# Query/key products token-major with 512 moving columns, turned afterwards by transposes

## The chip, the core and the metric

The kernel runs on one core of a Trainium2 chip. The engines are named as in the profile: PE (TensorE matmuls; PEld its weight loads), DVE (VectorE), ACT (ScalarE), POOL (GpSimd) and SP (SyncE, which issues most DMAs). Matmuls accumulate in PSUM, in banks of 128 partitions by 512 f32. The metric is the device time of one execution in microseconds; lower is better.

## What is computed

Two layers of a streaming encoder on 512 tokens of width 2048. Each layer normalises its input, multiplies it by one wide input projection, and splits the columns between a gated linear attention (GLA) group and a chunked softmax attention group of 8 heads:

```python
def hybrid_layer(x, w_in, w_out, ...):
    h = rmsnorm(x, g_pre)
    z = h @ w_in
    gq, gk, gv, gg, ga, aq, ak, av, ag = split_columns(z)
    ...
    o_att = chunk_band_attention(aq, ak, av, rel_bias)   # 8 heads of 128
    o_att = rmsnorm(o_att, g_att) * jax.nn.silu(ag)
    y = jnp.concatenate([o_gla, o_att], axis=-1) @ w_out
    return x + rmsnorm(y, g_post)
```

The change concerns `aq` and `ak`, the queries and keys of the softmax attention, 1024 columns each.

## The kernel before

**Two-term operands.** Each operand of a product is a rounded high part and a low rest, and each product is three matmuls: high by high, high by low, low by high. `split` (lines 108 to 110) makes the two parts of a tile: ACT writes the rounded copy (line 109), DVE the difference (line 110). `split_scaled` (from line 112) does so with a factor (lines 118 and 119).

**Blocks and pairs.** The weight columns are cut into blocks of 512. A query/key block holds the 256 query columns of two heads and then their 256 key columns; `QK01`, `QK23`, `QK45` and `QK67` are the four. `fast_gemm` (line 372) multiplies all 512 tokens by a pair of blocks with a scheme of seven products on quarters (Strassen's kind) in place of eight. `PAIRS[1]` is (QK01, QK23) and `PAIRS[2]` is (QK45, QK67), so each layer has two query/key calls and the kernel four (lines 1108 and 1109).

**Jobs.** A call runs 28 jobs: products P1 to P7, each over four chunks c of the 2048 inputs. A job is one chunk of 512 inputs, and `kk` runs over its two halves. For each job the weights are loaded, combined with another block where the product asks for it (DVE, lines 234, 236, 256), and split (ACT line 240, DVE line 250); `ahead()` prepares the coming jobs before a finished quarter is handed over. Then come the job's matmuls. After a product's last chunk, `copies` moves its accumulators out of PSUM (ACT, line 395), or `finished` hands a quarter over: `combine` returns a function that adds or subtracts two tiles on DVE (line 400) in place, in an `ev` buffer. P3, P7 and P2 hand over with a combination; P4 hands over its accumulator itself. Each handover comes in two parts of 128x512. The order of the last chunks in a call is P1, P5, P6, P3, P7, P2, P4; P7's is job 20 and P4's job 28.

**Two layouts.** With `feature_major=True`, which only the two query/key calls set, the weights are stationary and the tokens move: each job has 24 matmuls with 256 moving columns (line 435; 2 halves, 4 groups of 128 features, 3 terms). The result has features on partitions, as the attention scores need it, and the two parts of a quarter are its queries and its keys (`b` in `qk_consume`). In the other layout the tokens are stationary and the weights move: 12 matmuls with 512 moving columns (line 445; 2 halves, 2 token tiles, 3 terms), and the two parts are token tiles `t`.

**Query/key handover.** `qk_consume` (line 1087) takes a part, settles its combination, and splits it at 128x512 into the four tiles of its block: query high and low (scaled by `-QS`), key high and low. The last part of a block starts the attention of its two heads, by appending `attend` to `tasks`.

**Order of work.** `tasks` holds generators that run a step at a time; `delayed` holds functions that run after a count of steps. After each job, `Pace` advances them by `rate` steps (2.1 in the query/key calls). So attention runs in small steps between the jobs: scores (lines 976 to 978), the softmax (DVE 982, ACT 986), transposes of the probabilities (line 998, copied out by ACT line 1001 and DVE line 1003), the mix with the values (line 1015), and a last turn (line 1040). The instructions made in this order are then ordered for each engine by a planner, which keeps the dependencies, may put ready work of lower priority first, and assigns buffers from the pools. The pool `ps_ax` has four PSUM banks for everything that is not a product's accumulator (`aux()`), the pool of the accumulators four, and the `t2` temporaries have eight buffers.

**The product after it.** `PAIRS[3]` (linear attention's keys and queries) already runs token-major, and `transpose_q` turns its query quarters by four transposes through the identity (line 1119) with two ACT copies (line 1121).

Of the kernel before, what the change touches and what calls it, by code (L numbers as in the profile page):

```python
# [15 lines left out]
P = 128  # L16
# [10 lines left out]
QS = 128 ** -0.5  # L27
# [9 lines left out]
def hybrid_trunk(  # L37
# [14 lines left out]
    nc = tc.nc  # L52
# [38 lines left out]
    def aux():  # L91
        return ps_ax.tile([P, 512], F32, tag="ax", name=nm("ax"))
# [15 lines left out]
    def split(hi, lo, src):  # L108
        nc.scalar.copy(hi, src)
        return nc.vector.tensor_tensor(out=lo, in0=src, in1=hi.bitcast(F32), op=ALU.subtract).ins  # L110

    def split_scaled(hi, lo, src, scale, first=False):
        if first:
            first_high.append(
                nc.vector.tensor_scalar(out=hi, in0=src, scalar1=scale, scalar2=None, op0=ALU.mult).ins
            )
        else:
            nc.scalar.activation(hi, src, AF.Copy, scale=scale)
        nc.vector.scalar_tensor_tensor(
            out=lo, in0=src, scalar=scale, in1=hi.bitcast(F32), op0=ALU.mult, op1=ALU.subtract  # L120
        )
# [197 lines left out]
    def until(cond):  # L319
        while not cond():  # L320
            assert tasks or delayed
            pump(1)
# [46 lines left out]
    A = {}  # L369
    roles = ["XY", "YX"]  # L370

    def fast_gemm(l, pair, consume, rate=0.0, skip=0, feature_major=False, after=None, end=False, lag=0, ops=A, prod=None, acc=None):
        b0 = pair[0]
        gates = b0 == AG1
        wide = N1 if gates else W
# [42 lines left out]
        def matmuls(job, k, c, ts):  # L418
            a = job.a
            if a is None:  # L420
                key = {"P1": (0, 0, c), "P2": (1, 0, c), "P4": (1, 1, c)}.get(k) or (LEFT[k], c)
                until(lambda: key in ops)
                a = ops[key]
            out_ps = acc[target[k]]
            fresh = k in starts and c == 0
            apart = end and (k, c) in (("P7", 3), ("P4", 0))
            for kk, some in [(kk, (t,)) for t in ts for kk in range(2)] if apart else [(kk, ts) for kk in range(2)]:
                if feature_major:
                    for ft in range(4):
                        f = slice(ft * P, (ft + 1) * P)  # L430
                        tok = slice(kk * 256, (kk + 1) * 256)
                        dst = out_ps[ft // 2][:, (ft % 2) * 256 : (ft % 2 + 1) * 256]
                        terms = ((job.wh, 0), (job.wh, 1), (job.wl, 0))
                        for m, (lhs, part) in enumerate(terms):
                            nc.tensor.matmul(  # L435
                                dst, lhs[:, kk, f], a[:, part, tok],
                                start=(fresh and kk == 0 and m == 0 and ft % 2 == 0),
                                stop=(c == 3 and kk == 1 and m == 2), skip_group_check=True,
                            )
                else:  # L440
                    for t in some:
                        tok = slice(kk * 256 + t * P, kk * 256 + (t + 1) * P)
                        terms = ((0, job.wh), (0, job.wl), (1, job.wh))
                        for m, (part, rhs) in enumerate(terms):
                            last_mm[0] = nc.tensor.matmul(  # L445
                                out_ps[t], a[:, part, tok], rhs[:, kk, :],
                                start=(fresh and kk == 0 and m == 0),
                                stop=(c == 3 and kk == 1 and m == 2), skip_group_check=True,
                            ).ins

        for k, c in prod:
            if k == "P2" and (end or gates) and c == 0 or k == "P5" and parted and c == 0:
# [32 lines left out]
    def settled(src, comb):  # L485
        return src if comb is None else comb()
# [293 lines left out]
    def layer(l):  # L780
# [182 lines left out]
        class Head:  # L963
# [70 lines left out]
            def turn(self):  # L1034
                c, kk = self.hd // 2, self.hd % 2
                if kk == 0:
                    turned[c] = slot("g16", [2, 512], F32R)
                ps = aux()
                for t in range(NT):
                    nc.tensor.transpose(ps[:, t * P : (t + 1) * P], self.sg[:, t, :], ident)  # L1040
# [17 lines left out]
        def attend(hd, qk):  # L1058
            heads = {"a": Head(hd, qk, 0), "b": Head(hd + 1, qk, 1)}

            def turn(h):
                h.turn()
                if h.hd % 2:
                    heads_done.add(hd)

            for _ in range(5 if hd == HEADS[0] else 0):
                yield
            for step in ORDER:
                if step == "-":
# [12 lines left out]
                yield  # L1082
# [4 lines left out]
        def qk_consume(p):  # L1087
            sets = {}

            def f(j, h, b, src, comb):  # L1090
                if j not in sets:
                    if (p, j) == (1, 0):
                        until(lambda: 2 in heads_done)
                    sets[j] = [slot(tag, [2, 512], F32R) for tag in QKT[p, j]]
                z = settled(src, comb).rearrange("p (f n) -> p f n", f=2)
                hs = slice(h * 256, (h + 1) * 256)
                hi, lo = sets[j][2 * b][:, :, hs], sets[j][2 * b + 1][:, :, hs]
                if b == 0:
                    split_scaled(hi, lo, z, -QS)
                else:  # L1100
                    split(hi, lo, z)
                if h and b:
                    tasks.append(attend(4 * p + 2 * j, sets[j]))
            return f

        load_bias(0)
        load_bias(1)
        fast_gemm(l, PAIRS[1], qk_consume(0), rate=2.1, feature_major=True)
        fast_gemm(l, PAIRS[2], qk_consume(1), rate=2.1, feature_major=True)

        until(lambda: 0 in heads_done)
        tasks.insert(0, forget_gate_decay())
# [480 lines left out]
```

## Time and profile before

| | before |
|---|---|
| median of 3 runs | 1597.54 us (1596.91 to 1597.74) |
| profiled execution | 1597.99 us |
| its span, first to last instruction | 1596.1 us |
| TensorE clock granted, mean | 0.999 |
| matmuls | 9102 |
| query/key stage, layer 0 | about 176 to 369 us |
| query/key stage, layer 1 | about 967 to 1159 us |

In a row of a group stand the line, the engine, the operation, the tile it writes and the ones it reads, the shapes and the count; after the bar the group's busy time in us (overlaps counted once), the mean of one in ns, and the idle time of the engine just before them with what ended it. In a row of the timeline stand the start and the length in us; `x2` are two merged instructions, and a bracket gives idle time before it and its releaser. A row of the stretches gives, after the bounds and the length, each engine's busy time with the count of instructions, the granted clock, the share of the DMA engines and GB/s.

### The profile page before, as it was taken

The page shows a single profiled execution, that of the slowest core. Times are in us where ns is not written, and L with a number is a line of the kernel's source. Part 1 is how long each engine was busy: PE and PEld are TensorE (multiplying, and loading weights), DVE is VectorE, ACT ScalarE, POOL GpSimd, SP SyncE. Part 2 cuts the span into 40 slices and gives each one's busy share as a digit, 9 for nine tenths or more (in the row PEclk, how much of TensorE's full clock was granted, in tenths as well). Part 3 has the DMA queues.
Part 4 walks back from the last instruction along what each step waited for, and adds up shares of the span by engine and source line. Part 5 has one row for each costly group of instructions (what it writes and reads, how often), then busy time and mean ns, then how long its engine had stood idle before and what let it go on. Part 6 is the DMA issues. An engine that isn't in the chain of part 4 may idle for free.

```text
span 1596.1 us, 25037 instructions
## 1 busy us (share of the span) xinstructions
PE 1584.9 (99%) x9102; PEld 1369.8 (86%) x9102; DVE 1279.6 (80%) x1697; ACT 920.9 (58%) x1535; POOL 140.6 (9%) x222
## 2 busy tenths in 40 slices
PE   9999999999999999999999999999999999999998
PEld 7998999998888777888888899999988887788886
DVE  5978777678787877998989878775887878689887
ACT  7554445657464556664686456455675655566654
POOL 0220000001000011100122000000010000101001
PEclk9999999999999999999999999999999999999999
DMA  9798686685858769689879998847869586686887
GB/s 354 232 408 308 224 305 210 218 297 193 287 205 270 280 214 315 221 298 404 302 260 352 377 337 314 283 155 266 296 223 313 174 331 239 219 302 234 337 307 199
DMA packets 137739, 441.45 MB, mean 277 GB/s; under 512 B 15364, under 2 KB 27908, under 8 KB 137584
## 3 DMA queue, kind: packets, MB, share of 16 engines
q1 hardware_dynamic: 119952, 377.86, 66.2%
q0 software_dynamic: 17376, 61.70, 11.0%
q8 instruction: 72, 1.18, 0.3%
q14 instruction: 51, 0.42, 0.1%
q10 hardware_dynamic: 288, 0.30, 0.1%
HBM read 380.23 MB, written 61.62 MB: 277 GB/s over the span
## 4 chain that ended last, share of the span: by engine, by line
PE 91%; DVE 4%; DMA 3%; issue 1%; ACT 1%; POOLq 0%; DVEq 0%; ACTq 0%
PE mm L445 53%; PE mm L435 18%; PE mm L358 7%; PE ax L445 4%; DMA raw<-in_w_dram 3%; PE ax L1015 2%; DVE wl L250 2%; PE ax L1201 1%; PE ax L998 1%; PE ax L1173 1%; PE ax L978 1%; PE ax L977 1%; PE ax L976 1%; PE ax L1293 0%; DMA sa<-S 0%
## 5 line engine op out<-in xcount | busy, mean ns | idle before, releaser
L445 PE MATMUL mm<-wh,sa 128*128 128x512 f32 (+1 forms) x1600 | 506.1, 389 | 0.6 <-ACT wh L240 0.5
L240 ACT CAST wh<-H 128x1024 fp32r<-128x1024 f32 (+1 forms) x240 | 245.1, 1023 | 198.8 <-PE mm L445 86.2
L445 PEld LDWEIGHTS mm<-wh,sa 128*128 128x128 f32 x1600 | 298.1, 188 | 70.8 <-issue 6.9
L240 ACT CAST wh<-raw 128x1024 fp32r<-128x1024 f32 (+2 forms) x237 | 236.2, 1002 | 205.0 <-PE mm L445 84.2
L250 DVE TENSOR_TENSOR wl<-H,wh 128x1024 fp32r<-128x1024 f32 (+1 forms) x240 | 284.7, 1188 | 85.5 <-PE mm L445 37.8
L250 DVE TENSOR_TENSOR wl<-raw,wh 128x1024 fp32r<-128x1024 f32 (+2 forms) x237 | 272.8, 1156 | 55.4 <-PE mm L435 20.3
L445 PE MATMUL mm<-wl,sa 128*128 128x512 f32 (+1 forms) x800 | 310.3, 388 | 0.1
L435 PE MATMUL mm<-sa,wh 128*128 128x256 f32 x1280 | 237.7, 286 | 0.0
L445 PE MATMUL mm<-wh,a 128*128 128x512 f32 (+1 forms) x672 | 217.2, 389 | 0.0
L435 PEld LDWEIGHTS mm<-sa,wh 128*128 128x128 f32 x1280 | 200.5, 192 | 0.4
L435 PE MATMUL mm<-sa,wl 128*128 128x256 f32 x640 | 181.5, 284 | 0.1
L445 PEld LDWEIGHTS mm<-wl,sa 128*128 128x128 f32 x800 | 150.4, 188 | 29.5 <-DVE wl L250 0.9
L234 DVE TENSOR_TENSOR H<-H,raw 128x1024 f32<-128x1024 f32 (+1 forms) x136 | 161.4, 1189 | 1.5 <-DMA raw<-in_w_dram 0.9
L445 PEld LDWEIGHTS mm<-wh,a 128*128 128x128 f32 x672 | 125.1, 188 | 24.9
L445 PE MATMUL mm<-wl,a 128*128 128x512 f32 (+1 forms) x336 | 130.8, 390 | 0.5 <-DVE wl L250 0.5
L435 PEld LDWEIGHTS mm<-sa,wl 128*128 128x128 f32 x640 | 122.5, 192 | 0.4 <-DVE wl L250 0.3
L445 PE MATMUL mm<-wh,g 128*128 128x512 f32 (+1 forms) x416 | 120.5, 367 | 0.0
L489 POOL TENSOR_TENSOR sm<-sm,mhalf 128x2 f32<-128x2 f32 (+2 forms) x40 | 47.9, 1197 | 663.7 <-DVE sm L1025 364.9
L395 ACT COPY ev<-mm 128x512 f32<-128x512 f32 (+1 forms) x112 | 64.1, 572 | 57.4 <-PE mm L445 42.2
L435 PE MATMUL mm<-a,wh 128*128 128x256 f32 x512 | 94.8, 286 | 0.0
L236 DVE TENSOR_TENSOR raw<-H,raw 128x1024 f32<-128x1024 f32 (+1 forms) x52 | 61.5, 1184 | 35.8 <-DMA raw<-in_w_dram 35.6
L445 PEld LDWEIGHTS mm<-wh,g 128*128 128x128 f32 x416 | 75.4, 188 | 13.3 <-ACT ev L395 0.6
(276 smaller groups left out, 2436.3 us busy)
## 6 DMA issues: line engine op xcount, KB each, us to landing
raw<-in_w_dram SPq DMA_DIRECT2D x287, 512.0 KB, 5.2
sa<-S SPq DMA_DIRECT2D x188, 512.0 KB, 4.5
H<-in_w_dram SPq DMA_DIRECT2D x56, 512.0 KB, 5.0
sa<-A SPq DMA_DIRECT2D x48, 512.0 KB, 6.0
sa<-oS SPq DMA_DIRECT2D x32, 512.0 KB, 5.7
S<-g POOLq DMA_DIRECT2D x30, 512.0 KB, 8.0
raw<-in_w_ag_dram SPq DMA_DIRECT2D x32, 264.0 KB, 4.1
oS<-g POOLq DMA_DIRECT2D x16, 512.0 KB, 5.1
```

What stands on the lines that cost most here:

```text
L234: nc.vector.tensor_tensor(out=h, in0=h, in1=r, op=ALU.add)
L236: nc.vector.tensor_tensor(out=r, in0=h, in1=r, op=ALU.subtract)
L240: last_cast[0] = nc.scalar.copy(self.wh[:, z, :], src[:, z, :]).ins
L250: last_low[0] = nc.vector.tensor_tensor(out=self.wl[:, z, :], in0=self.src[:, z, :], in1=self.wh[:, z, :].bitcast(F32), op=ALU.subtract).ins
L358: nc.tensor.matmul(pss[o], a(part, kk, o) if callable(a) else a[:, part, t], rhs[:, kk, :], start=(i == 0 and kk == 0 and m == 0), stop=(i ...
L395: last_copy[0] = nc.scalar.copy(e, src[t]).ins
L435: nc.tensor.matmul(dst, lhs[:, kk, f], a[:, part, tok], start=(fresh and kk == 0 and m == 0 and ft % 2 == 0), stop=(c == 3 and kk == 1 and ...
L445: last_mm[0] = nc.tensor.matmul(out_ps[t], a[:, part, tok], rhs[:, kk, :], start=(fresh and kk == 0 and m == 0), stop=(c == 3 and kk == 1 ...
L489: nc.gpsimd.tensor_tensor(out=out_r, in0=v, in1=mhalf[:, : v.shape[-1]], op=ALU.pow)
L976: nc.tensor.matmul(ps[:, :n], self.qh[:, t], self.kh[:, :n], start=True, stop=False)
L977: nc.tensor.matmul(ps[:, :n], self.qh[:, t], self.kl[:, :n], start=False, stop=False)
L1015: nc.tensor.matmul(o, self.pt[i][:, j * P : (j + 1) * P], av[hd // 4, j // 2][:, j % 2, (hd % 4) * P : (hd % 4 + 1) * P], start=(j == 0), ...
```

## The change

The feature-major layout is taken out of `fast_gemm`; the query/key calls use the token-major one. In `qk_consume`, `f` now receives a token tile `t` of a quarter: with a combination it runs it, without one ACT copies the accumulator to a `t2` tile. It then delays `turn` by `1 + t` steps. `turn` takes an `ax` bank, turns the tile by four transposes of 128x128, and splits the query half and the key half of the result, 128x256 each, straight from PSUM. The last turn of a block starts its attention.

```diff
@@ fast_gemm, matmuls @@
-                if feature_major:
-                    for ft in range(4):
-                        f = slice(ft * P, (ft + 1) * P)
-                        tok = slice(kk * 256, (kk + 1) * 256)
-                        dst = out_ps[ft // 2][:, (ft % 2) * 256 : (ft % 2 + 1) * 256]
-                        terms = ((job.wh, 0), (job.wh, 1), (job.wl, 0))
-                        for m, (lhs, part) in enumerate(terms):
-                            nc.tensor.matmul(
-                                dst, lhs[:, kk, f], a[:, part, tok],
...
+                for t in some:
+                    tok = slice(kk * 256 + t * P, kk * 256 + (t + 1) * P)
+                    terms = ((0, job.wh), (0, job.wl), (1, job.wh))
+                    for m, (part, rhs) in enumerate(terms):
+                        last_mm[0] = nc.tensor.matmul(
+                            out_ps[t], a[:, part, tok], rhs[:, kk, :],
...
@@ qk_consume @@
-            def f(j, h, b, src, comb):
+            def turn(j, h, t, z):
                 if j not in sets:
-                    if (p, j) == (1, 0):
-                        until(lambda: 2 in heads_done)
                     sets[j] = [slot(tag, [2, 512], F32R) for tag in QKT[p, j]]
-                z = settled(src, comb).rearrange("p (f n) -> p f n", f=2)
-                hs = slice(h * 256, (h + 1) * 256)
-                hi, lo = sets[j][2 * b][:, :, hs], sets[j][2 * b + 1][:, :, hs]
-                if b == 0:
-                    split_scaled(hi, lo, z, -QS)
-                else:
-                    split(hi, lo, z)
-                if h and b:
+                ps = aux()
+                for i in range(4):
+                    nc.tensor.transpose(ps[:, i * P : (i + 1) * P], z[:, i * P : (i + 1) * P], ident)
+                tok = slice((2 * h + t) * P, (2 * h + t + 1) * P)
+                for b in range(2):
+                    hi, lo = sets[j][2 * b][:, :, tok], sets[j][2 * b + 1][:, :, tok]
+                    y = ps[:, b * 256 : (b + 1) * 256].rearrange("p (f n) -> p f n", f=2)
+                    if b == 0:
+                        split_scaled(hi, lo, y, -QS)
+                    else:
+                        split(hi, lo, y)
+                if h and t:
                     tasks.append(attend(4 * p + 2 * j, sets[j]))
+
+            def f(j, h, t, src, comb):
+                if j not in sets and (p, j) == (1, 0):
+                    until(lambda: 2 in heads_done)
+                if comb is None:
+                    z = t2()
+                    nc.scalar.copy(z, src)
+                else:
+                    z = comb()
+                delayed.append([1 + t, lambda: turn(j, h, t, z)])
             return f
...
-        fast_gemm(l, PAIRS[1], qk_consume(0), rate=2.1, feature_major=True)
-        fast_gemm(l, PAIRS[2], qk_consume(1), rate=2.1, feature_major=True)
+        fast_gemm(l, PAIRS[1], qk_consume(0), rate=2.1)
+        fast_gemm(l, PAIRS[2], qk_consume(1), rate=2.1)
```

More of the change, by code (lines that the diff above doesn't have):

```diff
@@ L370, in hybrid_trunk, with fast_gemm @@
     roles = ["XY", "YX"]
-    def fast_gemm(l, pair, consume, rate=0.0, skip=0, feature_major=False, after=None, end=False, lag=0, ops=A, prod=None, acc=None):
+    def fast_gemm(l, pair, consume, rate=0.0, skip=0, after=None, end=False, lag=0, ops=A, prod=None, acc=None):
         b0 = pair[0]
@@ L427, in matmuls @@
             for kk, some in [(kk, (t,)) for t in ts for kk in range(2)] if apart else [(kk, ts) for kk in range(2)]:
-                if feature_major:
-                    for ft in range(4):
-                        f = slice(ft * P, (ft + 1) * P)
-                        tok = slice(kk * 256, (kk + 1) * 256)
-                        dst = out_ps[ft // 2][:, (ft % 2) * 256 : (ft % 2 + 1) * 256]
-                        terms = ((job.wh, 0), (job.wh, 1), (job.wl, 0))
-                        for m, (lhs, part) in enumerate(terms):
-                            nc.tensor.matmul(
-                                dst, lhs[:, kk, f], a[:, part, tok],
-                                start=(fresh and kk == 0 and m == 0 and ft % 2 == 0),
-                                stop=(c == 3 and kk == 1 and m == 2), skip_group_check=True,
-                            )
-                else:
[L441 to L449, printed above, removed]
+                for t in some:
[4 more added lines that the diff above has]
+                            out_ps[t], a[:, part, tok], rhs[:, kk, :],
+                            start=(fresh and kk == 0 and m == 0),
+                            stop=(c == 3 and kk == 1 and m == 2), skip_group_check=True,
+                        ).ins
         for k, c in prod:
@@ L1088, in qk_consume @@
             sets = {}
-            def f(j, h, b, src, comb):
+            def turn(j, h, t, z):
                 if j not in sets:
-                    if (p, j) == (1, 0):
-                        until(lambda: 2 in heads_done)
                     sets[j] = [slot(tag, [2, 512], F32R) for tag in QKT[p, j]]
-                z = settled(src, comb).rearrange("p (f n) -> p f n", f=2)
-                hs = slice(h * 256, (h + 1) * 256)
-                hi, lo = sets[j][2 * b][:, :, hs], sets[j][2 * b + 1][:, :, hs]
-                if b == 0:
-                    split_scaled(hi, lo, z, -QS)
-                else:
-                    split(hi, lo, z)
-                if h and b:
-                    tasks.append(attend(4 * p + 2 * j, sets[j]))
+                ps = aux()
[10 more added lines that the diff above has]
+                if h and t:
+                    tasks.append(attend(4 * p + 2 * j, sets[j]))
+            def f(j, h, t, src, comb):
[4 more added lines that the diff above has]
+                    nc.scalar.copy(z, src)
+                else:
+                    z = comb()
+                delayed.append([1 + t, lambda: turn(j, h, t, z)])
             return f
```

## The prediction

> **What bounds the kernel now.** First the busy times and the clock on the page:
>
> ```profile
> PE 1584.9 (99%) x9102; PEld 1369.8 (86%) x9102; DVE 1279.6 (80%) x1697; ACT 920.9 (58%) x1535; POOL 140.6 (9%) x222
> PEclk9999999999999999999999999999999999999999
> ```
>
> PE is busy for 99% of the span at the full granted clock. A busy PE proves little by itself, because the profile models the ends of its matmuls, so the chain of work that ended last comes next:
>
> ```profile
> PE 91%; DVE 4%; DMA 3%; issue 1%; ACT 1%; POOLq 0%; DVEq 0%; ACTq 0%
> ```
>
> Ninety-one per cent of the chain is PE. The third view is the busy time by stretch; the first two rows are the query/key stages of the two layers, the only places the change touches:
>
> ```profile
> core 0: us, PE busy (x) PEld busy (x) DVE busy (x) ACT busy (x) POOL busy (x), PEclk, DMA share, GB/s
> 176.00:369.00 193.00, 191.55 (x1584) 190.44 (x1583) 141.16 (x207) 104.71 (x194) 7.62 (x10) 1.00 0.71 247
> 967.00:1159.00 192.00, 191.93 (x1588) 190.76 (x1587) 144.66 (x211) 106.60 (x198) 11.38 (x17) 1.00 0.73 257
> ```
>
> PE idles 1.5 us in the first and 0.1 us in the second, while DVE works 73 to 75% of the time, ACT 54 to 56%, and the DMA engines 0.71 to 0.73. So here PE's instructions set the time, and what the change is worth is how many PE instructions it drops and adds, each at its pace from start to start, and not at its printed duration.
>
> **Term 1, the products.** These are the groups of line 435:
>
> ```profile
> L435 PE MATMUL mm<-sa,wh 128*128 128x256 f32 x1280 | 237.7, 286 | 0.0
> L435 PE MATMUL mm<-sa,wl 128*128 128x256 f32 x640 | 181.5, 284 | 0.1
> L435 PE MATMUL mm<-a,wh 128*128 128x256 f32 x512 | 94.8, 286 | 0.0
> L435 PE MATMUL mm<-a,wl 128*128 128x256 f32 x256 | 72.3, 284 | 0.0
> ```
>
> The counts add up to 2688: 4 pairs of blocks, 28 jobs each, so 112 jobs of 24 matmuls. Line 445 does a job with 12 matmuls of 512 columns. The 286 ns is one matmul from its start to the modelled end, and neighbours overlap. The pace is read from the timeline, from its first and last row over a stretch without gaps; first line 435, then line 445 in an undisturbed stretch, then line 445 beside running attention:
>
> ```profile
> 195.81 0.40 PE L435 MATMUL mm<-sa,wh 128*128 128x256 f32 x2
> ...
> 202.64 0.40 PE L435 MATMUL mm<-sa,wh 128*128 128x256 f32 x2
> ```
>
> ```profile
> 139.65 0.39 PE L445 MATMUL mm<-wh,sa 128*128 128x512 f32 x1
> ...
> 146.91 0.39 PE L445 MATMUL mm<-wh,sa 128*128 128x512 f32 x1
> ```
>
> ```profile
> 458.35 0.63 PE L445 MATMUL mm<-wh,sa 128*128 128x512 f32 x2
> ...
> 460.66 0.39 PE L445 MATMUL mm<-wh,a 128*128 128x512 f32 x1
> ...
> 462.74 0.39 PE L445 MATMUL mm<-wl,a 128*128 128x512 f32 x1
> ...
> 463.65 0.39 PE L445 MATMUL mm<-wh,a 128*128 128x512 f32 x1
> ```
>
> From 195.81 to 202.64 start 57 matmuls: 6.83 / 57 = 119.8 ns. From 139.65 to 146.91 start 32: 226.9 ns. Beside attention ten start in 2.31 us (231 ns), a little later four in 0.91 us (228 ns). So 512 columns cost less than twice 256, because each matmul carries a charge that doesn't shrink with its columns. A job now costs 24 x 119.8 = 2875 ns. With 12 matmuls it costs 2723 ns at 226.9 and 2772 ns at 231. Over 112 jobs that saves 17.1 us at the quiet pace and 11.6 us at the slow one. I take 228 ns, nearest the quiet row, because no attention runs in the first 19 of each layer's 56 query/key jobs and beside attention both paces occur: 112 x (2875 - 2736) = **15.6 us saved**.
>
> The Trainium skill, page "TensorE: Matmul & The Clock Gate", section "Back-to-back issue gap", gives N/2.4 + 2.5 ns for warm matmuls, so 109.2 and 215.8 ns. By it the job would save 24 x 109.2 - 12 x 215.8 = 31 ns, 3.5 us in all as an estimate, and the change would lose. The rows above disagree: the charge beyond N/2.4 is about 13 ns here, at both widths, and the rows decide.
>
> **Term 2, the transposes.** Each pair hands over 8 halves of quarters (4 quarters, 2 token tiles), so `turn` runs 32 times with 4 transposes, 128 in all. The same operation, four turns of 128x128 f32 through the identity between line-435 matmuls, stands here:
>
> ```profile
> 337.70 0.29 PE L435 MATMUL mm<-sa,wl 128*128 128x256 f32 x1
> 337.83 0.60 PE L1040 MATMUL ax<-cst,sg 128*128 128x128 f32 x4
> 338.18 0.49 PE L435 MATMUL mm<-a,wh 128*128 128x256 f32 x2
> 338.51 0.28 PE L435 MATMUL mm<-a,wl 128*128 128x256 f32 x1
> ```
>
> Three line-435 matmuls and the four transposes lie between 337.70 and 338.51: 0.81 - 3 x 0.12 = 0.45 us for the four. (The next matmul's record starts early, at 338.18, but the one after it is late by the same; only the stretch over both counts.) 32 x 0.45 = **14.4 us added**.
>
> **Term 3, ACT and DVE.** The operands were split straight from the quarter, at 128x512; now they are split from the turned tile as two halves of 128x256, and the last quarter, which needs no combination, is first copied by ACT. The first four rows are today's splits in the first layer's stage, the fifth the copy of an accumulator, the last two are 128x256 work out of PSUM elsewhere:
>
> ```profile
> L118 ACT ACTIVATE g<-ev 128x512 fp32r<-128x512 f32 x6 | 3.8, 627 | 5.6 <-DVE ev L400 5.6
> L109 ACT CAST g<-ev 128x512 fp32r<-128x512 f32 x6 | 3.7, 621 | 2.4 <-DVE ev L400 2.4
> L119 DVE SCALAR_TENSOR_TENSOR g<-ev,g 128x512 fp32r<-128x512 f32 x6 | 4.0, 674 | 0.0
> L110 DVE TENSOR_TENSOR g<-ev,g 128x512 fp32r<-128x512 f32 x6 | 4.1, 684 | 0.0
> L395 ACT COPY ev<-mm 128x512 f32<-128x512 f32 x12 | 7.0, 582 | 7.4 <-PE mm L435 7.4
> L1121 ACT ACTIVATE g<-ax 128x256 f32<-128x256 f32 x16 | 5.0, 384 | 0.0
> L1188 DVE SCALAR_TENSOR_TENSOR g<-g,a_end,ax 128x256 f32<-128x256 f32 x56 | 26.8, 479 | 2.0
> ```
>
> Per pair ACT goes from 8 x 0.62 = 5.0 us to 16 x 0.38 + 2 x 0.58 = 7.3, and DVE from 8 x 0.68 = 5.4 to 16 x 0.48 = 7.7. That is 4.6 us more on each in a stage of 193 us, where ACT has 88 us free and DVE 52. I cost it at nothing; the products of PE hide it. Without that cover it would cost at most these 9.2 us in both layers.
>
> **The new waits.** The transposes wait for the combination on DVE (line 400) or the copy on ACT, which wait for the quarter's last matmul. PE takes its matmuls in the order that the planner fixed, so whatever matmuls of the next job come after the transposes in that order stand behind them while they wait. The nearest row is the same pattern in the key/query product that follows: combination, four transposes, split.
>
> ```profile
> L1119 PE MATMUL ax<-cst,ev 128*128 128x128 f32 x32 | 4.5, 272 | 0.0
> ```
>
> Eight such groups of four, no idle time before any. Against it stands the one stall of the stage, 1.45 us of PE:
>
> ```profile
> 325.71 1.23 DVE L256 TENSOR_TENSOR H<-H,raw 128x1024 f32<-128x1024 f32 x1 [4.71 <-DMA raw<-in_w_dram]
> ...
> 331.29 0.55 DVE L1003 COPY t<-ax 128x384 f32<-128x384 f32 x1
> ...
> 331.99 0.91 PE L1015 MATMUL ax<-g,t 128*128 128x128 f32 x6 [1.45 <-DVE t L1003]
> ```
>
> A weight block landed late, DVE waited 4.7 us with everything behind it, and PE stood before attention matmuls whose input DVE had not copied. So a new wait is bounded by nothing and 1.45 us; I take nothing, by the nearest row (the same pattern), and keep the other end.
>
> Each turned tile also takes one of the four `ax` banks for about two ACT and two DVE reads (1.7 us). If banks run short, attention's steps come later while PE has products to run: no cost on PE. No DMA moves, and the loads of the next jobs are issued ahead of the handover as before; a job with its share of transposes is 2736 + 129 = 2865 ns against 2875, so the weights have the same time to land. `turn` starts attention one step later; its work is unchanged.
>
> **The sum.** -15.6 + 14.4 = -1.2 us. The profiled execution took 1597.99 us (span 1596.1 and 1.9 around it), 0.45 above the median of the runs. Off the median: 1597.5 - 1.2 = **1596.3 us**. With 226.9 ns the sum is -2.7 (1594.8), with 231 ns +2.8 (1600.3). About 0.2%, 3.2 us, is what a measurement of this kernel can tell from no change.
>
> **Rivals.**
>
> - *Faster.* The quiet pace holds beside attention (-2.7), and the 1.45 us stall goes, since the steps around it shift; the second layer's stage, with the same code, idles only 0.1 us. -4.1: 1593.4. For: that row. Against: 231 ns beside attention, and nothing in the change removes late weights.
> - *Slower: DVE late at the turns.* Quarters finish where P7 and P2 prepare weights on DVE from just-landed blocks, the place of the quoted stall. Each turn caught costs 1.45 us. With -1.2 from the work, four of the 32 turns bring it past +3.2; at five it is -1.2 + 7.3: 1603.6. For: the stall exists, and 32 new places can catch it. Against: one stall among the many waits of attention on DVE and ACT today, and none at line 1119.
> - *Halving the count doesn't pay.* If a 512-column matmul cost two of 256 in this stage (239.6 ns), the transposes would be all that's left: +14.4, 1611.9. Against: no row above reaches 239.6. The skill's formula quoted above comes close to this case, and the trace doesn't bear it out.
>
> **How the numbers follow.** Forecast 0.60, faster 0.18, late turns 0.20, no saving 0.02. So faster by over 0.2% 0.18, within 0.2% 0.60, slower 0.22. The range runs from 1592.5, just past the faster case, to 1604.0, through late turns at its price of five; it leaves out more than five late turns and no saving, and covers the paces from 226.9 to 231.
>
> **What would show it.** Line 435 gone and line 445 up by 1344 matmuls of 512 columns, at 227 to 231 ns in these stages; 128 new 128x128 transposes, about 0.45 us for each four; idle PE before them near 0; the two stages together 1 to 3 us shorter. Idle time before the transposes put down to DVE would show the second rival; a pace near 240 ns the third. A change of more than 3 us outside the two stages would mean that I missed a way in which they reach the rest.

## The result, and the profile after

| | before | after |
|---|---|---|
| median, measured side by side (6 runs each) | 1597.78 us (1596.91 to 1600.03) | 1603.93 us (1602.95 to 1606.34) |
| ratio to before | 1 | 1.0037 [1.0025, 1.0050] |
| span of the profiled execution | 1596.1 us | 1604.6 us |

The changed kernel is slower by 0.37%, some 6 us, where no change that can be told (-1.2 us) was forecast. Its page shows the busy times and the chain that ended last:

```profile
PE 1587.9 (99%) x7886; PEld 1310.8 (82%) x7886; DVE 1282.6 (80%) x1729; ACT 926.8 (58%) x1575; POOL 142.2 (9%) x222
PE 91%; DVE 5%; issue 1%; DMA 1%; ACT 1%; SPq 0%; POOLq 0%; DVEq 0%; ACTq 0%
```

PE still shows 99% and 91%: as read from the page, nothing has happened. There are 9102 - 7886 = 1216 matmuls fewer, which is 1344 product matmuls fewer and 128 transposes more. What the changed query/key stages hold also reads as forecast. The timeline of PE in a stretch without attention (first and last row), and the groups of the first layer's stage (176 to 369 us):

```profile
188.70 0.62 PE L432 MATMUL mm<-wh,sa 128*128 128x512 f32 x2
...
205.70 0.62 PE L432 MATMUL mm<-wh,sa 128*128 128x512 f32 x2
```

```profile
L1082 PE MATMUL ax<-cst,ev 128*128 128x128 f32 x44 | 6.6, 272 | 0.0
...
L119 DVE SCALAR_TENSOR_TENSOR g<-ax,g 128x256 fp32r<-128x256 f32 x12 | 4.8, 405 | 0.5 <-ACT g L118 0.5
L118 ACT ACTIVATE g<-ax 128x256 fp32r<-128x256 f32 x12 | 4.6, 380 | 2.8 <-PE ax L1082 2.8
```

Between the two starts lie 75 matmuls: 17.00 / 75 = 226.7 ns, the quiet pace. The transposes have no idle time put down in front of them.

So where did the time go? The products are the same work in both kernels if a 256-column one is counted as half. So the stages can be set side by side by the start of each stage's first product, found by counting:

```
first product of           before    after   after - before
query/key pair 1, layer 0   176.4     176.7    +0.3
query/key pair 2, layer 0   263.5     261.1    -2.4
key/query product, layer 0  368.9     360.3    -8.6
value product, layer 0      460.7     454.1    -6.5
product after it, layer 0   549.7     553.1    +3.4
key/query product, layer 1 1159.3    1155.2    -4.1
value product, layer 1     1251.1    1249.1    -2.0
product after it, layer 1  1340.1    1348.1    +8.0
span                       1596.1    1604.6    +8.4
```

The -8.6 is mostly not a gain: attention, which runs between the products, is later in the changed kernel and is done in the later stages. Work moved out of one stage comes back in another. Only where attention is over, at the product after the value product, can the two be compared. There the changed kernel is 3.4 us late in layer 0 and 8.0 in both layers together, and from there on the two kernels run in step. (The profiled execution of the changed kernel, 1606.34 us, is the slowest of its six; by the medians the loss is 6.2 us.) The loss shows in the head of the value stage. The stretches of before, then of after:

```profile
core 0: us, PE busy (x) PEld busy (x) DVE busy (x) ACT busy (x) POOL busy (x), PEclk, DMA share, GB/s
454.00:480.00 26.00, 26.00 (x143) 22.31 (x142) 24.25 (x39) 14.97 (x36) 1.03 (x1) 1.00 0.42 147
1249.00:1275.00 26.00, 26.00 (x138) 22.15 (x137) 23.89 (x35) 15.20 (x35) 1.24 (x2) 1.00 0.40 136
```

```profile
454.00:480.00 26.00, 24.14 (x143) 20.25 (x142) 23.16 (x47) 17.80 (x51) 2.19 (x3) 1.00 0.41 146
1249.00:1275.00 26.00, 24.14 (x143) 20.24 (x142) 23.16 (x47) 17.80 (x51) 2.19 (x3) 1.00 0.42 148
```

PE has no idle time before and 1.86 us after, in each layer, at the full clock and with the DMA engines at 0.41 to 0.42. The timeline of PE in that window shows what it idles between:

```profile
471.08 0.39 PE L432 MATMUL mm<-wh,a 128*128 128x512 f32 x1
471.31 0.33 PE L963 MATMUL ax<-g,g 128*128 128x384 f32 x1
...
473.03 0.33 PE L985 MATMUL ax<-cst,t 128*128 128x128 f32 x1 [0.47 <-DVE sm L969]
...
475.33 0.49 PE L1002 MATMUL ax<-g,t 128*128 128x128 f32 x2
476.75 1.16 PE L1002 MATMUL ax<-g,t 128*128 128x128 f32 x8 [0.93 <-ACT t L988]
...
478.37 0.94 PE L1002 MATMUL ax<-g,t 128*128 128x128 f32 x6
479.06 0.48 PE L432 MATMUL mm<-wh,sa 128*128 128x512 f32 x1
```

From 471.31 to 479.06 PE runs no product at all, only the tail of attention (scores, transposes, mix), whose steps wait for one another through DVE and ACT. The printed gaps understate it: between the starts at 475.33 and 476.75 two matmuls ran, 0.2 us of work in 1.4. The product that comes at 479.06 is the value stage's second one. The row on DVE that ends just ahead of it stands first here, the same instruction of the kernel before second, and the first product of the changed kernel's value stage (PE) third:

```profile
477.27 1.28 DVE L1139 TENSOR_TENSOR t<-mm,g 128x512 f32<-128x512 f32 x2
```

```profile
474.50 1.28 DVE L1140 TENSOR_TENSOR t<-mm,g 128x512 f32<-128x512 f32 x2
```

```profile
454.13 0.39 PE L432 MATMUL mm<-wh,a 128*128 128x512 f32 x1
```

The DVE instruction reads P4's quarter of the key/query product out of the accumulators (`mm`), multiplies it by the decay and writes it to a `t2` tile (`t`). Until it has run, two of the four accumulator banks stay taken. The value stage's first product has the other two, and its second one must wait. Before, the instruction starts 474.5 - 460.7 = 13.8 us after the first product of the stage; after, 477.3 - 454.1 = 23.2 us after it.

The same shape stands at the head of the key/query stage, where the new copy of P4's quarter comes late. PE, then ACT:

```profile
360.05 0.39 PE L432 MATMUL mm<-wh,sa 128*128 128x512 f32 x1
```

```profile
373.35 0.38 ACT L118 ACTIVATE g<-ax 128x256 fp32r<-128x256 f32 x1 [0.71 <-PE ax L1082]
374.17 1.05 ACT L240 CAST wh<-H 128x1024 fp32r<-128x1024 f32 x1 [0.43 <-PE mm L432]
375.12 1.07 ACT L1099 COPY t<-mm 128x512 f32<-128x512 f32 x2
```

P4's last matmul starts at 360.05, and the copy of its result at 375.12, 15 us later, though ACT had idle time in between (0.71 and 0.43 us here). It too writes a `t2` tile. Three suspects follow from this: the `ax` banks, the `t2` tiles, and the accumulators held meanwhile.

### The profile page after: what moved, and what is told of

Same layout as the page of the kernel before. It is cut to its first block, busy times and chain, and to the rows that moved or that the text cites. A ratio compares the mean times of both kernels' runs of the same rounds, so it can differ in the third digit from the quotient of the medians.

```text
span 1604.6 us, 22662 instructions
## 1 busy us (share of the span) xinstructions
PE 1587.9 (99%) x7886; PEld 1310.8 (82%) x7886; DVE 1282.6 (80%) x1729; ACT 926.8 (58%) x1575; POOL 142.2 (9%) x222
## 3 DMA queue, kind: packets, MB, share of 16 engines
q0 software_dynamic: 17376, 61.70, 10.9%
## 4 chain that ended last, share of the span: by engine, by line
PE 91%; DVE 5%; issue 1%; DMA 1%; ACT 1%; SPq 0%; POOLq 0%; DVEq 0%; ACTq 0%
PE mm L432 71%; PE mm L358 6%; PE ax L432 4%; PE ax L1002 2%; DVE wl L250 1%; PE ax L1200 1%; PE ax L985 1%; PE ax L1172 1%; PE ax L1082 1%; DVE H L234 1%; PE ax L963 1%; DMA raw<-in_w_dram 1%; PE ax L965 1%; PE ax L964 1%; DVE g L110 0%
## 5 line engine op out<-in xcount | busy, mean ns | idle before, releaser
L432 PE MATMUL mm<-wh,sa 128*128 128x512 f32 (+1 forms) x2240 | 712.3, 390 | 0.8 <-ACT wh L240 0.5
L432 PEld LDWEIGHTS mm<-wh,sa 128*128 128x128 f32 x2240 | 416.6, 188 | 94.6 <-issue 8.1
L432 PE MATMUL mm<-wl,sa 128*128 128x512 f32 (+1 forms) x1120 | 435.4, 389 | 2.2 <-DVE wl L250 2.2
L432 PE MATMUL mm<-wh,a 128*128 128x512 f32 (+1 forms) x928 | 302.3, 391 | 0.0
L432 PEld LDWEIGHTS mm<-wl,sa 128*128 128x128 f32 x1120 | 210.4, 188 | 44.2 <-DVE wl L250 3.9
L432 PEld LDWEIGHTS mm<-wh,a 128*128 128x128 f32 x928 | 172.2, 188 | 33.9
L432 PE MATMUL mm<-wl,a 128*128 128x512 f32 (+1 forms) x464 | 181.4, 391 | 0.5 <-DVE wl L250 0.5
L234 DVE TENSOR_TENSOR H<-H,raw 128x1024 f32<-128x1024 f32 (+1 forms) x136 | 161.3, 1188 | 2.0 <-DMA raw<-in_w_dram 1.0
L432 PEld LDWEIGHTS mm<-wl,a 128*128 128x128 f32 x464 | 87.2, 188 | 17.6 <-DVE wl L250 0.7
L432 PEld LDWEIGHTS mm<-wh,g 128*128 128x128 f32 x416 | 75.2, 188 | 13.7 <-ACT wh L240 0.9
L432 PE MATMUL mm<-wl,g 128*128 128x512 f32 (+1 forms) x208 | 75.8, 366 | 0.0
L256 DVE TENSOR_TENSOR H<-H,raw 128x1024 f32<-128x1024 f32 (+1 forms) x44 | 51.6, 1175 | 28.0 <-DMA raw<-in_w_dram 27.6
L240 ACT CAST wh<-g 128x1024 fp32r<-128x1024 f32 x36 | 37.9, 1060 | 31.3 <-PE mm L432 14.9
```

Of the source, the lines that this page charges most:

```text
L234: nc.vector.tensor_tensor(out=h, in0=h, in1=r, op=ALU.add)
L240: last_cast[0] = nc.scalar.copy(self.wh[:, z, :], src[:, z, :]).ins
L256: nc.vector.tensor_tensor(out=h, in0=h, in1=self.src, op=ALU.add)
L432: last_mm[0] = nc.tensor.matmul(out_ps[t], a[:, part, tok], rhs[:, kk, :], start=(fresh and kk == 0 and m == 0), stop=(c == 3 and kk == 1 ...
```

## The experiments

Times are medians; a ratio is to the kernel before, run beside it on the same chip, with its 95% interval.

**The turns taken out.** Each turned tile is replaced by the unturned one, so the 128 transposes and their banks are left out, queries and keys stay token-major, and the scores are those of other operands.

```diff
-                ps = aux()
-                for i in range(4):
-                    nc.tensor.transpose(ps[:, i * P : (i + 1) * P], z[:, i * P : (i + 1) * P], ident)
...
-                    y = ps[:, b * 256 : (b + 1) * 256].rearrange("p (f n) -> p f n", f=2)
+                    y = z[:, b * 256 : (b + 1) * 256].rearrange("p (f n) -> p f n", f=2)
```

> The changed kernel without its 128 transposes and without the ax banks they take: the halves are split at 128x256 from the settled quarter itself, unturned, so the scores are those of other operands, with the same instructions. Theory held back (the turned tiles hold attention back, by their banks or the extra hop, and its tail then stalls PE at the head of the value stage): the 14.4 us of transposes go and the stall of about 8 to 10 us of both layers with them, so about 1580 us, and the first scores start about 2 us earlier. Rival, order (the planner's order is worse for any change of the products, whatever the turns do): only the 14.4 us go, about 1589.5, and the value stages stay at 99 us.

Measured: 1581.54 us beside 1597.94, ratio 0.9899 [0.9883, 0.9916]. This is what the theory expected. The products alone are 16.4 us faster (by the interval of the ratio, 13 to 19). The turns then cost about 1603.93 - 1581.54 = 22.4 us (two runs that did not stand side by side), of which 14.4 is PE's transposes by the forecast's price: 8 us are something else. And the copy is on time here, in the same `t2` tile (timeline of ACT):

```profile
360.26 1.07 ACT L1096 COPY t<-mm 128x512 f32<-128x512 f32 x2
```

**Attention later in the kernel before.** Its first step waits four steps longer.

```diff
-            for _ in range(5 if hd == HEADS[0] else 0):
+            for _ in range(9 if hd == HEADS[0] else 0):
```

> The kernel before with attention begun 9 steps after its operands instead of 5, which is 4 steps, about 2 jobs or 5.5 us, later; nothing else. Theory late tail (attention that runs late costs time by itself, in the value stage): 1597.5 plus 4 to 8 us, value stages at 93 us or more against 89. Rival, order: lateness of this size is hidden by the products, 1597.5 within 1.5 us.

Measured: 1600.14 us, ratio 1.0017 [1.0008, 1.0026], some 2.7 us by the ratio, between the two expectations. The cost is in another place: the stretches show the head of the value stage full and a stall at 415 to 430 us. The timelines of DVE and PE (second and third fence) put its 1.88 us to a DVE that had itself waited 3.38 us for a weight block, so this run doesn't show that late attention costs by itself:

```profile
415.00:430.00 15.00, 13.12 (x73) 10.75 (x72) 11.62 (x19) 7.34 (x15) 1.03 (x1) 1.00 0.74 248
454.00:480.00 26.00, 26.00 (x145) 22.38 (x144) 24.25 (x38) 16.17 (x37) 1.03 (x1) 1.00 0.48 167
```

```profile
423.50 1.23 DVE L256 TENSOR_TENSOR H<-H,raw 128x1024 f32<-128x1024 f32 x1 [3.38 <-DMA raw<-in_w_dram]
```

```profile
425.81 0.33 PE L998 MATMUL ax<-cst,t 128*128 128x128 f32 x1 [1.88 <-DVE sg L1029]
```

**Attention denser, or earlier, in the changed kernel.** First the rate of steps in the two query/key calls, then the number of empty first steps:

```diff
-        fast_gemm(l, PAIRS[1], qk_consume(0), rate=2.1)
-        fast_gemm(l, PAIRS[2], qk_consume(1), rate=2.1)
+        fast_gemm(l, PAIRS[1], qk_consume(0), rate=2.5)
+        fast_gemm(l, PAIRS[2], qk_consume(1), rate=2.5)
```

> The changed kernel with 2.5 in place of 2.1 steps of attention after each query/key job. Theory late tail: attention catches up by about 20 steps over 56 jobs, the tail leaves the value stage, 1596 to 1599 us, value stages back at about 89 to 91 us. Theory held back by banks: the steps stand earlier in the program, but they still wait for banks, so less comes back, 1600 to 1603. Rival, order: 1604 within 2 us.

```diff
-            for _ in range(5 if hd == HEADS[0] else 0):
+            for _ in range(1 if hd == HEADS[0] else 0):
```

> The changed kernel with attention begun 1 step after its operands instead of 5, at the same rate. Theory late tail: the 4 steps that attention gains are about 5.5 us, half of its delay of some 10 us, 1598 to 1601 us. Held back by banks: 1602 to 1604. Rival, order: 1604 within 2 us.

Measured: 1611.14 us, ratio 1.0089 [1.0073, 1.0105], and 1605.80 us, ratio 1.0053 [1.0038, 1.0068]. Neither mends anything; the denser steps make it 7 us worse. So "attention is too late, make it earlier in the program" was not the remedy. PE's timeline in the denser kernel names the wait:

```profile
375.90 1.16 PE L1002 MATMUL ax<-g,t 128*128 128x128 f32 x8 [1.92 <-ACT t L988]
...
383.53 0.66 PE L1082 MATMUL ax<-cst,t 128*128 128x128 f32 x4 [1.59 <-ACT t L1099]
```

The second row is the turn of P4's quarter, which stands on PE waiting for the late copy of line 1099. Here the copy comes 23.5 us after the first product of its stage (359.4; ACT's timeline). With attention earlier it comes 19.2 us after it (378.6 against 359.4), the turn again stands waiting for it (PE's timeline), and the value stage's head keeps most of its idle time:

```profile
382.87 1.10 ACT L1099 COPY t<-mm 128x512 f32<-128x512 f32 x2
```

```profile
379.26 0.66 PE L1082 MATMUL ax<-cst,t 128*128 128x128 f32 x4 [2.15 <-ACT t L1099]
```

```profile
454.00:480.00 26.00, 24.70 (x147) 21.09 (x147) 24.27 (x43) 18.34 (x48) 2.20 (x3) 1.00 0.43 149
```

**Fewer turns in the `ax` banks.** P3, P2 and P4 are turned into the accumulator bank that their quarter left, and P4's copy goes into an `ev` tile; only P7's turns take `ax` banks.

```diff
-            def turn(j, h, t, z):
+            def turn(j, h, t, z, bank):
...
-                ps = aux()
+                ps = aux() if bank is None else bank
...
-                    z = t2()
+                    z = ev()
```

> The changed kernel, but a turn of P3, P2 or P4 writes its four transposes into the accumulator bank that its quarter just left, not into a new ax bank, and the copy of P4 goes to an ev buffer; only the 8 turns of P7, whose accumulator lives on, still take an ax bank. The work on every engine is the same. Theory line (ax banks are handed out in the order in which the program makes them, so turns wait behind attention's tiles and attention behind the turns): 24 of 32 turns leave the line, 1596 to 1600 us, value stages at 90 to 95 us against 99. Rival, work (the turns cost their extra 8 us through PE, ACT and DVE time or the extra hop, whatever bank they take): 1602 to 1606, value stages at 99.

Measured: 1604.18 us, ratio 1.0048 [1.0032, 1.0065]. The time is the rival's, but the value stage takes 88 us, less than the 90 to 95 of the theory, so neither expectation held. The head of the value stage is full (first row), but the turns now hold accumulators and PE stands elsewhere, before a turn that waits for the combination on DVE (second fence, PE's timeline; lines 1084 and 401 there are 1082 and 400 of the changed kernel):

```profile
454.00:480.00 26.00, 26.00 (x136) 22.02 (x135) 23.74 (x37) 12.92 (x29) 3.02 (x1) 1.00 0.41 142
```

```profile
233.07 0.66 PE L1084 MATMUL ax<-cst,ev 128*128 128x128 f32 x4 [1.19 <-DVE ev L401]
```

One loss went and another came. Two edits went together here, so the next run makes one of them alone.

**Only the copy's tile.** The changed kernel with one word replaced:

```diff
-                    z = t2()
+                    z = ev()
                     nc.scalar.copy(z, src)
```

> The changed kernel with the copy of P4's quarter in an ev buffer instead of a t2 one, nothing else. Theory line: t2 buffers are handed out in order too, but only 8 of 32 handovers need one, so 0 to 2 us less than the changed kernel, 1602 to 1604. Rival, t2 is the line that counts: the copies that came 15 us after their last matmul come within 2 us, and 1597 to 1600.

Measured: 1597.27 us beside 1597.50, ratio 0.9996 [0.9988, 1.0005]. The whole loss is gone. ACT's timeline, then DVE's:

```profile
362.72 0.58 ACT L1099 COPY ev<-mm 128x512 f32<-128x512 f32 x1
...
366.40 0.58 ACT L1099 COPY ev<-mm 128x512 f32<-128x512 f32 x1
```

```profile
475.20 1.28 DVE L1139 TENSOR_TENSOR t<-mm,g 128x512 f32<-128x512 f32 x2
```

The halves are copied at 362.7 and 366.4, 2.4 us before and 1.3 us after the first product of the next stage (365.1); in the changed kernel it was 15 us after it (375.1, 360.3). The gated keys, whose tile was not touched, come at 475.2, and as the value stage starts at 461.5 here, that is 13.7 us into it, as before the change. So a late copy looks like one way in which the end of attention, and with it the keys, becomes late. But the planner orders everything anew for each edit, and from 261 us on this kernel's order differs from the changed kernel's in more than the copy.

**The transposes alone, in the kernel before.** The 24 parts that have a combination are turned into an `ax` bank (96 transposes) and the result is thrown away after ACT has read one column; operands and products are as before.

```diff
+        def idle_turn(z):
+            ps = aux()
+            for i in range(4):
+                nc.tensor.transpose(ps[:, i * P : (i + 1) * P], z[:, i * P : (i + 1) * P], ident)
+            nc.scalar.copy(sm(1), ps[:, 0:1])
...
+                if comb is not None:
+                    delayed.append([1 + b, lambda z=z: idle_turn(z)])
```

> The kernel before with 4 transposes of each combined quarter half into an ax bank, delayed by 1 or 2 steps as in the change, and thrown away after an ACT read of one column: 24 turns, 96 transposes, 10.6 us of PE, while the operands are still split from the quarter at once. If turned tiles in the line hold attention back by themselves: 1598 + 10.6 + 3 to 8, so 1612 to 1617 us. If only the operands' own wait in the line does harm: 1607 to 1610.

Measured: 1607.98 us, ratio 1.0063 [1.0049, 1.0078], 10 us (6.3 thousandths of 1597.5). That is 96 transposes at the forecast's 0.45 us for four: 10.8 us. The interval is 8 to 12 us. So the turns' price on PE is borne out, and turned tiles in the `ax` banks cost nothing beyond it that can be told as long as nothing waits for them.

**The gated keys' tile, and both.** By the timeline the idle time sits where the gated keys hold the accumulators. If so, freeing them must mend the kernel even with the copy left late. First this line alone, then it and the copy's, then both with rate 2.5:

```diff
-            z = kd if comb is not None else t2()
+            z = kd if comb is not None else ev()
             nc.vector.tensor_tensor(out=z, in0=kd, in1=decay[h][:, t, :], op=ALU.mult)
```

> The changed kernel with the copy of P4's quarter still in a t2 tile; only the gated keys at the head of the value stage (line 1138) go into an ev tile. Theory 'line of t2 tiles', in its wide form: both handovers of a P4 quarter harm by the same line, so the value stage (98.97 us after, 89.05 before) falls to 93 to 96 us and the time to 1598-1601 us. Rival 'one late copy': the wait at the value stage's head is only the consequence of attention that the late copy of the query/key quarter has pushed back; then the value stage stays above 97 us and the time within 1602.5-1605 us.

> The changed kernel with both: the copy of P4's quarter and the gated keys in ev tiles. Wide form of the theory: both lines are gone and the time goes below the 1597.27 us of the run with the copy alone, to 1594.5-1596.5 us, since 4.6 and 3.6 us of excess are left in the key stage there. Rival 'one late copy': nothing is left to gain at the value stage's head (it was 88.60 us with the copy alone), 1596.8-1597.8 us.

> The kernel with both ev tiles and attention's steps at rate 2.5 instead of 2.1 in the query/key stages. With the t2 copy, rate 2.5 cost 7.2 us more than rate 2.1 (1611.14 against 1603.93), in stalls of 2 to 4.7 us at 373-382 us. If those stalls were the late copy's too, they go, and the time is within 1594-1599 us. If denser steps wait for one another whatever the copy's tile is (softmax to transposes, lines 969 to 985), most of the cost stays: 1601-1606 us.

Measured, beside 1598.03 us: 1598.57 us, ratio 1.0002 [0.9991, 1.0012]; 1598.69 us, 1.0002 [0.9994, 1.0011]; 1599.86 us, 1.0010 [0.9999, 1.0021]. The gated keys' tile alone is enough. DVE's timeline and the stretches of that kernel:

```profile
455.09 0.68 DVE L1139 TENSOR_TENSOR ev<-mm,g 128x512 f32<-128x512 f32 x1
...
460.51 0.68 DVE L1139 TENSOR_TENSOR ev<-mm,g 128x512 f32<-128x512 f32 x1
```

```profile
454.00:480.00 26.00, 26.00 (x141) 22.11 (x140) 24.28 (x39) 16.41 (x36) 1.16 (x2) 1.00 0.56 178
1249.00:1275.00 26.00, 26.00 (x142) 22.11 (x141) 23.16 (x32) 17.71 (x40) 1.16 (x2) 1.00 0.52 167
```

The keys come 1.6 us after the stage's first product (453.5) instead of 23.2, PE is full in both windows, and the product after the value product starts at 549.2, where it started at 553.1: 3.9 us saved in layer 0, 7.9 by the same place in layer 1 (1340.2 instead of 1348.1). The late copy is still there (374.3 us, 14.9 after the first product of its stage) and, alone, costs nothing that can be told: PE is full around it.

```profile
371.00:384.00 13.00, 13.00 (x72) 10.99 (x71) 11.45 (x21) 8.93 (x22) 0.00 (x0) 1.00 0.27 82
```

This run isolates the keys: on PE, ACT and DVE its instructions stand in the same order as in the changed kernel up to the first microseconds of the value stage, where the keys now come. The rival "one late copy", that the wait at the value stage's head only follows and can't be mended there, falls.

Both tiles together gave no more than either: the expected 1594.5 to 1596.5 was a miss. With either, the loss is already gone, so there is nothing to add. The denser steps, 7.2 us worse with the `t2` copy, are 1.2 us worse without it (1599.86 against 1598.69, slightly above what was expected): the stretch in which the denser kernel stood, here first with the `t2` tiles and then with the `ev` tiles, has filled up.

```profile
371.00:384.00 13.00, 9.43 (x65) 7.96 (x64) 9.38 (x27) 11.25 (x37) 1.01 (x1) 1.00 0.27 81
```

```profile
371.00:384.00 13.00, 13.00 (x67) 10.93 (x66) 11.25 (x21) 8.59 (x19) 0.00 (x0) 1.00 0.45 141
```

**Copy and idle turns without the new products.** The kernel with idle turns again, and P4's quarter copied into a `t2` tile and split from there:

```diff
-                z = settled(src, comb)
-                if comb is not None:
+                if comb is None:
+                    z = t2()
+                    nc.scalar.copy(z, src)
+                else:
+                    z = comb()
                     delayed.append([1 + b, lambda z=z: idle_turn(z)])
```

> The kernel before (feature-major products, 256 columns) with the 96 idle transposes of P3, P2 and P7 as in e7 and, new, P4's quarter copied by ScalarE into a t2 tile and split from there, as the changed kernel copies it. e7 took 1607.98 us. Theory 'late copy': tiles of the turns in the ax line make attention later, and a copy in the t2 line behind attention holds the accumulators; the two together harm whatever form the products have: 1611-1615 us, with the copy 5 us or more behind P4's last product. Rival 'the token-major products themselves make it' (their quarter ends late or their pace differs): the copy comes within 2 us of the product's end, as it did without transposes (e1), and the time stays at 1607.5-1609.5 us.

Measured: 1607.94 us, ratio 1.0062 [1.0048, 1.0075], the same as without the copy (1607.98). The theory's expectation failed. ACT's timeline shows the copy on time, the key/query stage starting at 373.2 us:

```profile
372.34 0.59 ACT L1103 COPY t<-mm 128x512 f32<-128x512 f32 x1 [1.20 <-PE mm L435]
374.89 0.56 ACT L1103 COPY t<-mm 128x512 f32<-128x512 f32 x1
```

So a `t2` copy and turned tiles are not enough to make the copy late; nor are a `t2` copy and token-major products, as the run without turns shows. What this run leaves out is that in the changed kernel attention itself waits for the turns, and that the products are token-major. Whether it takes the first alone or both was not tried.

**Two controls.** The gated keys in `ev` in the kernel before (the edit above, nothing else), and the changed kernel once more on the same chip.

> The kernel before, with the gated keys of P4's quarter (line 1139 there) in ev instead of t2, nothing else. In the kernel before they come 13.8 us after the first product of the value stage and no stall follows; in the changed kernel they came 23.2 us after it, and there the ev tile brought some 5 us. If that wait costs only where it outlasts the products that can run beside it, nothing is gained here: ratio to the kernel before within 0.9985-1.0015 though the keys come within 5 us of the stage's start. If the tile is a gain of its own, which would have been there without the change, the ratio is below 0.998 (3 us or more).

> The changed kernel itself once more, beside the run above on the same chip: the result of its comparison was 1603.93 us, ratio 1.0037, and this chip should give 1.0025-1.0050 again; only if it does can the ratios near 1.000 of the runs with ev tiles be put down to the tiles and not to the chip.

Measured, beside 1598.69 us: 1598.67 us, ratio 1.0000 [0.9991, 1.0009], though the first of P4's keys came at 462.4 us, 0.3 us into the stage (first row, DVE's timeline); and 1606.27 us, ratio 1.0042 [1.0030, 1.0054]. The tile is no gain of its own: a wait of 13.8 us there is free, one of 23.2 is not. And the changed kernel's loss is the same on this chip, down to the window (second fence):

```profile
462.37 0.68 DVE L1140 TENSOR_TENSOR ev<-mm,g 128x512 f32<-128x512 f32 x1
```

```profile
454.00:480.00 26.00, 24.14 (x143) 20.25 (x142) 23.16 (x47) 17.80 (x51) 2.19 (x3) 1.00 0.40 145
1249.00:1275.00 26.00, 24.14 (x143) 20.22 (x143) 23.16 (x45) 17.70 (x51) 2.19 (x3) 1.00 0.43 150
```

No version that turns its operands beat the kernel before by more than the measurement tells; the best are level with it.

## Why the prediction was wrong

**The products** are borne out: 15.6 us forecast (11.6 to 17.1), 16.4 measured with the turns out (13 to 19 by the interval; that run also splits from SBUF instead of PSUM). The quiet stretch runs at 226.7 ns. By the rule of the Trainium skill, page "TensorE: Matmul & The Clock Gate", section "Back-to-back issue gap", only 3.5 us would have come; the run doesn't agree with it. The section calls this formula the gap of an isolated matmul, which the prediction left out.

**The transposes** are borne out as far as tried: 14.4 us were forecast for 128, and 96 of them by themselves cost 10 us (8 to 12) where this price gives 10.8.

**ACT and DVE** got less extra work than the forecast gave them: over the whole kernel ACT is busy 5.9 us longer (926.8 against 920.9) and DVE 3.0 us (1282.6 against 1279.6), where 9.2 each were forecast.

**The sum of the work** is borne out within its error: once either `t2` tile is out of the way, the kernel is level with before (0.9996 [0.9988, 1.0005]), and -1.2 us is a ratio of 0.9992.

**The new waits** is the step that failed. It said: "If banks run short, attention's steps come later while PE has products to run: no cost on PE." It bounded a wait by 1.45 us at a turn, and it priced P4's copy, in the step before, only by ACT's 0.58 us. In place of no cost, PE stands 1.86 us at the head of each layer's value stage, and the keys' tile alone makes up the whole difference. Three things were missed there.

- The copy needs a tile as well as an engine. It asks for `t2` tiles, which attention uses too, and came 15 us into the next stage; in `ev` its second half started 1.3 us into it. While it waits, a finished quarter keeps its accumulators.
- Later attention moves its tail, and the gated keys stand behind that tail: `until(lambda: 6 in heads_done)` in `kq_consume` makes the rest of heads 6 and 7 first and begins 4 and 5, and by the time that the keys of P4's quarter ask for their `t2` tile, all but the last steps of 4 and 5 have asked for theirs. So the keys come late too, and with them the accumulators for the value stage's second product.
- "PE has products to run" holds only while a free pair of accumulators is there. The first product of the value stage is 48 matmuls, 10.9 us at 226.7 ns. Before, it and the steps of attention between them filled PE from 460.7 to 476.2 us, so keys that came 13.8 us into the stage cost nothing; at 23.2 us PE has run out, and only attention's tail is left, step by step.

The price: by the kernel with the keys' tile alone, 3.9 us in layer 0 and 7.9 in both, and 5.4 us by the medians (1603.93 - 1598.57, not run side by side; by the ratios 0.0035 x 1598 = 5.6). With the forecast's -1.2 from the work, that gives +4.2 to +6.7, and 6.2 was measured. The 5.4 is no independent check, since the kernel with the keys' tile is level with the kernel before.

**The rivals.** The slower case forecast, DVE late at the turns, gives nearly the same time (1603.6) by another mechanism. It isn't what happened, so it is luck that the measured 1603.93 us lies just inside the range, which ends at 1604.0 for that case: the groups of the changed stage put no idle time before the transposes. It did appear in the run with the accumulator banks, 1.19 us before a turn. The faster case and the case that halving the count doesn't pay are not borne out.

**What would show it.** The last sentence of the prediction was the one that told: a change of more than 3 us outside the two stages. It is in the key/query and value stages. The sign "the two stages together 1 to 3 us shorter" failed with it: they are 8.9 and 7.6 us shorter, mostly because part of attention left them (80 matmuls of the mix stand in each instead of 98), and the two stages after them together are 12 us longer in each layer.

**What the copy waited for.** In the changed kernel the first half of the copy is given the buffer of a tile of turned probabilities, which the mix on PE is the last to read (first row), and the second half the buffer of the tile that line 1008 writes after this mix (second row, ACT):

```profile
371.35 0.83 PE L1002 MATMUL ax<-g,t 128*128 128x128 f32 x6
```

```profile
372.28 0.28 ACT L1008 ACTIVATE t<-ax 128x128 bf16<-128x128 f32 x1 [0.77 <-PE ax L1002]
```

So the tiles are free at 372.2 and 372.6 us, some 12 us after P4's last product. The rest, to 375.12, is ACT's own order: lines 118 and 240, each waiting for PE, stand before the copy. With the turns out the first half gets the buffer of the same tile, but there the mix begins at 358.85, 1.4 us before the copy.

**What stays open.** The copy is late because that mix begins 11.3 us after P4's last product; with the turns out it is 0.2 us. Why attention falls so far behind only with real turns, whether by waiting for them alone or together with the token-major products, stays open.

## What to carry to other kernels

When an edit adds a copy out of an accumulator, ask which pool its tile comes from, who else draws on that pool, and what the accumulator holds up meanwhile; a pool shared with a long, late consumer is a wait. Work that is "hidden beside PE" is hidden only as long as PE has products whose accumulators are free, so a delay has to be followed to the next place where it meets the main work, even when that is a hundred microseconds on. And compare two kernels at a place where the work that moves between stages is over, not stage by stage.

## What the runs showed that was not expected

- A late handover is free up to a point. Gated keys 1.6, 13.7 and 13.8 us into the value stage cost nothing that can be told; at 21.8 us (attention begun earlier) PE lacks 1.30 of 26.00 us there, at 23.2 us 1.86. The copy shows the like in the stage before: 14.9 us into it, it is free; at 19.2 us (attention begun earlier) and 23.5 us (denser) the turn of the copied tile holds up PE for 2.15 and 1.59 us.
- The idle time repeats exactly: PE is busy 24.14 of 26.00 us in both layers and in both profiles of the changed kernel, though single times of the kernel before ranged from 1595.06 to 1604.11 us beside the runs with `ev` tiles.
- Two mends of one loss don't add (ratios 1.0002 and 0.9996 alone, 1.0002 together). In the stretches of the kernel with both, PE has 13.48 us of 15.00 between 505 and 520 us with the DMA share at 1.00; whether late weights set the end there was not tried.
